# Attention logits on the two halves of TensorE's rows, with the decay added by VectorE

## The chip, the cores and the metric

The kernel runs on one core of one Trainium2 chip. A core has a matrix engine (TensorE, PE in the profile; PEld is its loading of weights), a vector engine (VectorE, DVE), a scalar engine (ScalarE, ACT), GpSimd (POOL) and SyncE (SP, which here issues most of the DMAs). TensorE reads SBUF and writes PSUM, a memory of banks of 512 f32 columns; VectorE and ScalarE read PSUM and clear it for the next use. Each engine works through its own queue in order and waits on semaphores.

The metric is device time in microseconds, the median over runs of the whole kernel.

## The reference

Two layers over 1024 positions of width 1024, each with a pre-norm and a residual, then a final norm. The first is an RG-LRU layer. The second, which the change concerns, is attention with a forget gate, 16 heads of 64:

```python
q, k, v = ...                      # (1024, 16, 64) each, from h @ w_in
f_logit = u[..., 4 * 1024:] + b_f  # one gate value per position and head
cum = jnp.cumsum(jax.nn.log_sigmoid(f_logit), axis=1)
logits = einsum("bqhd,bkhd->bhqk", q, k) / 8
logits = logits + (cum[query] - cum[key])
logits = where(key <= query, logits, -1e30)
p = softmax(logits)
y = einsum("bhqk,bkhd->bqhd", p, v) * silu(gate)
x = x + y @ w_out
```

The term `cum[query]` is the same for all keys of a query, so it drops out of a softmax that subtracts the row's maximum; only `-cum[key]` matters.

## The kernel before

Every f32 operand of a product is split in two: `hi`, the value rounded to the type that TensorE multiplies at full pace (f32r), and `lo`, the rest (`to_hi`, `to_lo`). A product of two split operands is the sum of three: hi by hi, hi by lo, lo by hi. The projections (`gemm_steps`) issue these three for each of 8 blocks of the contraction, 512 columns at a time, into one PSUM bank. All products go through the helper at L54, so in the profile they are told apart by tile names: `gps` (projections), `ups` and `ops`, `vps` (values), `S` (logits), `pt` (transposes of p), `O` (weighted sums), `turn` (the last stage).

Attention goes head by head. The queries and keys of a pair of heads come out of `kq_units` as `qkh` and `qkl`, [128 x 1024], two heads on 64 partitions each. `load` and `load_q` copy one head's part by DMA, from SBUF to SBUF, into two sets of operands that alternate by head:

- `T[s]`, the keys, [128, 2, 1024]. Slab 0 has hi on rows 0 to 63 and lo on rows 64 to 127. Slab 1 has hi again on rows 0 to 63, and on rows 64 to 67 two rows of ones and the two parts of `cum`.
- `U[s][c]`, the queries of half c of the sequence, [128, 2, 512]. Slab 0 has hi on both halves of the rows. Slab 1 has lo on rows 0 to 63, and on rows 64 to 67 the two parts of `cum` and two rows of minus one.

`cum` is computed in `forget`, half by half, split into hi and lo by VectorE, and kept in DRAM (`cumd`). `fixed_rows` sets the constant rows once.

`maxima(hd, c)` makes the logits of four blocks of 128 queries. Block i has n = 128(i+1) keys, and they go into a PSUM tile `S` of two banks (tag "S", two buffers, which the transposes `pt` use too) in one or two pieces of 256 columns or more, each the sum of two products: slab 0 with all 128 rows (hi by hi and hi by lo), slab 1 with 96 rows (lo by hi, and the decay). Then VectorE (L715) adds a bf16 mask of n columns, negates, and finds the row's minimum `m`, all in one instruction, and ScalarE (L720) writes p = exp(-S + m) to SBUF with its row sums. `weigh(hd, c)` later transposes p on TensorE (L58), splits it (`ph` by ScalarE, `pl` by VectorE) and multiplies it with the values.

The order of the work is written by hand. `run(order, ...)` reads a string: 0 is a step of `weigh`, 1 a block of `maxima`, and a dot is a step of `fill`, six 512-column products of the projections for the next pair (in the last heads, of the output projection), as in `ORDER = "1.0.1.1.1.0.0", "10.1.0.1.01.0.0"`. Each step is issued behind the last product of the step before. `load(hd + 2)` stands at the end of head hd's steps. The last stage, `turned`, takes the buffers of `T`, `U` and `U0`, `U1` for its results, and a buffer "xp" for squares.

Of the kernel before, what the change touches and what calls it, by code (L numbers as in the profile page):

```python
# [11 lines left out]
F32 = mybir.dt.float32  # L12
# [5 lines left out]
P = 128  # L18
# [20 lines left out]
def trunk(ctx: ExitStack, tc: tile.TileContext, xt, w0, wg, wo0, pc, gn, gf, w1, wv, wf, bf, wo1, out):  # L39
# [33 lines left out]
    for _ in range(10):  # L73
        matmul(warm[:, :P], onesf, onesf, start=True, stop=True)

    pct = const.tile([P, 8, NB], F32, name="pct")
    gnt = const.tile([P, 2, KT], F32, name="gnt")
    cw = [pct[:, j] for j in range(4)]
    cb, ba, bx, ap_ = (pct[:, j] for j in range(4, 8))


    def to_hi(hi, src, eng, scale=None):
# [99 lines left out]
    late = ctx.enter_context(ExitStack())  # L182
    with ExitStack() as l0:
        xpool = l0.enter_context(pool("x", 1))
        ypool = l0.enter_context(pool("y", 2 * GROUP))
        lru = l0.enter_context(ExitStack())
        tmp = lru.enter_context(pool("t0", 1, side="right"))
# [6 lines left out]
            return tmp.tile([P, SEQ], dtype, tag=tag, name=tag, bufs=bufs)  # L194


        sm = const
        c2 = sm.tile([P, NB], F32, name="c2")
        nc2 = sm.tile([P, NB], F32, name="nc2")
        e_ = sm.tile([P, NB], F32, name="sp_e")  # L200
# [285 lines left out]


    y1d = dram.tile([2, KT, P, HALF], F32, name="y1d")
    cumd = dram.tile([HEADS, 2, SEQ], F32, name="cumd")
    recd = dram.tile([HEADS, 8, P], F32, name="recd")  # L490

    with ExitStack() as l1:
# [2 lines left out]

        T = [tu.tile([P, 2, SEQ], F32R, tag=f"T{s}", name=f"T{s}") for s in range(2)]

        U0 = tu.tile([P, 2, HALF], F32R, tag="U", name="U")  # L500
        U = [(U0, tu.tile([P, 2, HALF], F32R, tag=f"U{s}", name=f"U{s}")) for s in range(2)]

        def fixed_rows():
            for s in range(2):
                nc.gpsimd.memset(f32(T[s][64:, 1]), 1.0)
                for u in U[s][s:]:
                    nc.vector.memset(f32(u[64:, 1]), 0.0)
                    nc.vector.memset(f32(u[64:68, 1]), -1.0)

        def project(w, use, hs=(0, 1)):  # L510

# [87 lines left out]
        def load(hd, cs=slice(0, SEQ), us=(0, 1)):  # L599

            pair, s = hd // 2, hd % 2
            rows = slice(s * HD, (s + 1) * HD)
            hi, lo = (f32(z[rows, cs]) for z in kq[pair, 1])
            nc.sync.dma_start(f32(T[s][:64, 0, cs]), hi)
            nc.sync.dma_start(f32(T[s][:64, 1, cs]), hi)
            nc.sync.dma_start(f32(T[s][64:, 0, cs]), lo)
            nc.sync.dma_start(f32(T[s][66:68, 1, cs]), cumd[hd, :, cs])
            for c in us:
                load_q(hd, c)

        def load_q(hd, c):
            s = hd % 2
            u = U[s][c]
            hi, lo = (f32(z[s * HD : (s + 1) * HD, halves[c]]) for z in kq[hd // 2, 0])
            nc.sync.dma_start(f32(u[:64, 0]), hi)
            nc.sync.dma_start(f32(u[64:, 0]), hi)
            nc.sync.dma_start(f32(u[:64, 1]), lo)
            nc.sync.dma_start(f32(u[64:66, 1]), cumd[hd, :, halves[c]])


        drain(kq_units(0, ((1, (0,)), (0, (0,)))))
# [3 lines left out]
        Vs = {}  # L625
        bft = const.tile([HEADS, 1], F32, name="bft")
        nc.sync.dma_start(bft, bf)
        unit = at.tile([HEADS, HALF], F32, tag="recb", name="unit", bufs=1)
        nc.gpsimd.memset(unit, 1.0)
        cum = at.tile([HEADS, SEQ], F32, tag="sg", name="cum")  # L630

        def forget(half):
            cs = slice(half * HALF, (half + 1) * HALF)
            pt = ps.tile([P, HALF], F32, tag="O", name="fps")
            for i in range(4):
                if half and i > 1:
                    yield
                with tc.issue_after(pe[0].ins):
                    transpose(pt[:HEADS, i * P : (i + 1) * P], fz[:, half * 4 + i], ident)
            z_, e_ = (at.tile([HEADS, HALF], F32, tag=t, name=n, bufs=3) for t, n in (("ph", "z"), ("pl", "e")))  # L640
            parts = [at.tile([HEADS, HALF], F32R, tag=f"p{i + 2 * half}", name="cp", bufs=1) for i in (3, 4)]
            hi, lo = parts
            nc.scalar.activation(z_, pt[:HEADS], AF.Identity, bias=bft)
            nc.vector.scalar_tensor_tensor(e_, z_, -1.0, z_, ALU.mult, ALU.min)
            nc.scalar.activation(e_, e_, AF.Exp)
            nc.scalar.activation(e_, e_, AF.Ln, bias=1.0)
            nc.vector.scalar_tensor_tensor(z_, z_, 0.0, e_, ALU.min, ALU.subtract)
            nc.vector.tensor_tensor_scan(
                cum[:, cs], unit, z_, cum[:, HALF - 1 : HALF] if half else 0.0, ALU.mult, ALU.add
            )  # L650
            to_hi(hi, cum[:, cs], nc.vector)
            to_lo(lo, cum[:, cs], hi, nc.vector)
            for i in range(2):
                nc.sync.dma_start(cumd[:, i, cs], f32(parts[i]))
            for hd in range(2):
                if half == 0:
                    load(hd, cs, (0,) if hd == 0 else ())
# [2 lines left out]
        next(first)  # L660
        next(first)

        fixed_rows()

        mask = tu.tile([P, SEQ], BF16, name="mask")
        nc.gpsimd.memset(mask, 0.0)
        nc.gpsimd.affine_select(
            out=mask, in_=mask, pattern=[[-1, SEQ]], compare_op=ALU.is_ge, fill=NEG, base=SEQ - P, channel_multiplier=1
        )

        take(first, 8)
# [20 lines left out]
        def maxima(hd, c):  # L692

            s = hd % 2
            pair = hd // 2
            if c == 0:
                stats[hd] = at.tile([P, 8], F32, tag="sums", name="sums")
            sums = stats[hd]
            for i in range(4 * c, 4 * c + 4):
                n = (i + 1) * P  # L700

                o_ = 192 if i == 4 else 0
                S = ps.tile([P, SEQ], F32, tag="S", name="S")[:, o_:]
                u = U[s][c]
                qs = slice(i % 4 * P, i % 4 * P + P)
                for lo_, hi_ in ((0, min(n, HALF - o_)), (HALF - o_, n)):
                    if hi_ <= lo_:
                        continue
                    hi_ = max(hi_, lo_ + 256)
                    matmul(S[:, lo_:hi_], u[:, 0, qs], T[s][:, 0, lo_:hi_], start=True, stop=False)  # L710
                    matmul(
                        S[:, lo_:hi_], u[:96, 1, qs], T[s][:96, 1, lo_:hi_], start=False, stop=True
                    )
                m = at.tile([P, 1], F32, tag="m", name="m", bufs=4)
                nc.vector.tensor_tensor_reduce(  # L715
                    S[:, :n], S[:, :n], mask[:, SEQ - n :], -1.0, -NEG, ALU.add, ALU.min, accum_out=m
                )

                p = ps_[i] = at.tile([P, n], F32, tag=f"p{i}", name="p", bufs=1)
                seen[0] = nc.scalar.activation(  # L720
                    p, S[:, :n], AF.Exp, bias=m, scale=-1.0, accum_out=sums[:, i : i + 1]
                )
                yield
            if hd == HEADS - 1 or c == 1:
                b0, b1 = (4 * c if hd == HEADS - 1 else 0), 4 * c + 4
                nb = b1 - b0
                sums = sums[:, b0:b1]
                nc.vector.tensor_scalar(sums, sums, 2.0, None, ALU.mult)
                nc.vector.reciprocal(sums, sums)
                tr = ps.tile([P, P], F32, tag="O", name="tr")  # L730
                nc.tensor.transpose(tr[:nb], sums, ident)
                rc = at.tile([8, P], F32, tag="rc", name="rc", bufs=1)
                nc.vector.tensor_copy(rc[:nb], tr[:nb])
                nc.gpsimd.dma_start(recd[hd, b0:b1], rc[:nb])
                if s == 0:
                    recs[pair] = at.tile([P, SEQ], F32, tag="recb", name="recb", bufs=1)
                rows = slice(s * HD, (s + 1) * HD)
                nc.gpsimd.dma_start(
                    recs[pair][rows, b0 * P : b1 * P],
                    recd[hd : hd + 1, b0:b1].rearrange("o b q -> o (b q)").to_broadcast([HD, nb * P]),  # L740
                )
                yield
# [155 lines left out]
        def turned(c, q):  # L898
# [2 lines left out]
            xs = left.pop((c, q), None) or residual(c, q)  # L901

            if c == 0:
                res = tu.tile([P, 2, SEQ], F32, tag=f"T{q}", name="res")
                res = [res[:, b] for b in range(2)]
            elif q == 0:
                res = [tu.tile([P, SEQ], F32, tag=t, name="res") for t in ("U", "U0")]
            else:
                res = [tu.tile([P, SEQ], F32, tag="U1", name="res"), at.tile([P, SEQ], F32, tag="p7", name="res", bufs=1)]
            for b in range(2):  # L910
# [4 lines left out]
                for h, (d0, nd) in enumerate(parts):  # L915
# [6 lines left out]
                    for k in range(2):  # L922
# [4 lines left out]
                        matmul(pt, yh, wl, start=False, stop=k == 1)  # L927
                        if k == 0:
                            yield
                    sq = at.tile([P, HALF], F32, tag="xp", name="sq1", bufs=2)[:, : nd * P]  # L930
                    nc.scalar.activation(sq, pt, AF.Square, accum_out=ss[:, min(h, ss.shape[1] - 1)].unsqueeze(1))
                    if c == 0 or h < len(parts) - 1:
                        nc.vector.tensor_tensor(res[b][:, hs], pt, grow[:, hs], ALU.mult)
# [189 lines left out]
```

## Time and profile before

| | |
|---|---|
| median of 3 runs | 1125.76 us (1124.42 to 1128.13) |
| the profiled execution, first to last instruction | 1127.7 us |
| TensorE busy | 1114.3 us, 99% |
| VectorE busy | 758.6 us, 67% |
| ScalarE busy | 589.3 us, 52% |
| GpSimd busy | 195.6 us, 17% |
| granted TensorE clock, mean | 0.998 |
| first and last product into S start at | 504.2 and 1072.7 us |

The profile is one execution, recorded by the hardware; its span lies inside the range of the runs, 1.9 us above their median. In a row of a group, the first number behind the bar is the time in which at least one of the group ran, then follows the mean length of one in ns, then the engine's idle time ahead of the group and what ended it. Products are pipelined and their ends are modelled, so two of them overlap in the record; their starts tell the pace.

### The profile page before, as it was taken

How to read it: one execution, taken by the hardware profiler on the slowest of the kernel's cores; microseconds unless marked ns; L12 is line 12 of the kernel's file. 1: busy time of each engine (PE TensorE's matmuls, PEld its weight loads, DVE VectorE, ACT ScalarE, POOL GpSimd, SP SyncE). 2: the span in 40 equal slices, each digit the busy share in tenths (PEclk: the TensorE clock that was granted, in tenths of full speed). 3: DMA queues.
4: the chain of work that ended last, by engine and by line, in shares of the span. 5: the costliest groups of instructions: out<-in, count | busy, mean ns of one | idle time of the engine just before them, and what ended most of it. 6: DMA issues, size and time to landing. Idle time of an engine off the chain costs nothing.

```text
span 1127.7 us, 15774 instructions
## 1 busy us (share of the span) xinstructions
PE 1114.3 (99%) x5691; PEld 936.8 (83%) x5691; DVE 758.6 (67%) x1268; ACT 589.3 (52%) x1081; POOL 195.6 (17%) x155
## 2 busy tenths in 40 slices
PE   9999999999999999999999999999999999999997
PEld 7788888888888887988888988889888898888786
DVE  7888755776568789656676466664667646676545
ACT  8488345355453656365555355553555535644335
POOL 1322112221121201431021110212102110021220
PEclk9999999999999999999999999999999999999999
DMA  6111111111111114433425224242252422564345
GB/s 235 57 47 42 51 52 52 38 58 45 52 38 52 47 44 145 129 112 102 112 71 123 66 77 117 72 118 71 74 119 73 118 71 77 176 189 158 117 154 187
DMA packets 62902, 105.43 MB, mean 93 GB/s; under 512 B 9796, under 2 KB 24772, under 8 KB 62824
## 3 DMA queue, kind: packets, MB, share of 16 engines
q1 hardware_dynamic: 59704, 95.97, 28.9%
q0 software_dynamic: 3120, 8.46, 2.3%
q8 instruction: 45, 0.74, 0.3%
q14 instruction: 33, 0.27, 0.1%
HBM read 63.30 MB, written 15.93 MB: 70 GB/s over the span
## 4 chain that ended last, share of the span: by engine, by line
PE 92%; DMA 2%; DVE 2%; issue 1%; ACT 1%; SPq 1%; POOL 0%; DVEq 0%; POOLq 0%; ACTq 0%
PE gps L54 33%; PE ops L54 16%; PE ups L54 12%; PE vps L54 8%; PE S L54 6%; PE O L54 6%; PE pt L58 5%; PE gate L54 3%; PE turn L54 3%; DMA wf<-in_wo 1%; DMA x<-in_xt 1%; POOL wl L96 0%; PE rsrow L54 0%; DMA wf<-in_w 0%; DMA yhl<-y1d 0%
## 5 line engine op out<-in xcount | busy, mean ns | idle before, releaser
L54 PE MATMUL gps<-hh,wh 128*128 128x512 f32 x576 | 229.1, 398 | 0.6 <-DVE qkl L595 0.6
L54 PE MATMUL gps<-hh,wl 128*128 128x512 f32 x576 | 226.8, 394 | 0.0
L54 PE MATMUL gps<-hl,wh 128*128 128x512 f32 x576 | 226.7, 394 | 0.0
L85 ACT CAST wh<-wf 128x512 fp32r<-128x512 f32 (+2 forms) x156 | 94.2, 607 | 147.8 <-PE ops L54 55.3
L96 POOL TENSOR_TENSOR wl<-wf,wh 128x512 fp32r<-128x512 f32 (+1 forms) x60 | 101.0, 1689 | 389.8 <-ACT wh L85 362.5
L720 ACT ACTIVATE p<-S,m 128x128 f32<-128x128 f32 (+7 forms) x128 | 94.8, 741 | 137.9 <-DVE m L715 136.8
L96 DVE TENSOR_TENSOR pl<-pt,ph 128x512 fp32r<-128x512 f32 (+1 forms) x198 | 98.7, 540 | 88.1 <-ACT ph L85 87.6
L54 PEld LDWEIGHTS gps<-hl,wh 128*128 128x128 f32 x576 | 108.3, 188 | 24.7 <-issue 0.5
L54 PEld LDWEIGHTS gps<-hh,wh 128*128 128x128 f32 x576 | 108.6, 189 | 20.5 <-DVE qkl L595 0.8
L54 PEld LDWEIGHTS gps<-hh,wl 128*128 128x128 f32 x576 | 108.7, 189 | 20.1 <-POOL wl L96 0.6
L715 DVE CUSTOM_DVE_ANT_0 S<-S,mask 128x128 f32<-128x128 f32 (+7 forms) x128 | 97.3, 761 | 28.8 <-PE S L54 28.8
L85 ACT CAST ph<-pt 128x512 fp32r<-128x512 f32 (+1 forms) x198 | 83.6, 473 | 36.2 <-PE pt L58 28.9
L54 PE MATMUL S<-T,U 96*128 96x512 f32 (+7 forms) x384 | 91.9, 348 | 2.7 <-ACT p L720 2.7
L96 DVE TENSOR_TENSOR wl<-wf,wh 128x512 fp32r<-128x512 f32 x96 | 70.7, 741 | 28.3 <-ACT wh L85 27.4
L381 DVE TENSOR_TENSOR x<-x,ops 128x512 f32<-128x512 f32 x80 | 54.1, 683 | 48.0 <-PE ops L54 48.0
L54 PEld LDWEIGHTS S<-T,U 128*128 128x128 f32 (+1 forms) x384 | 68.6, 190 | 16.1 <-ACT p L720 3.5
L58 PE MATMUL pt<-ident,p 128*128 128x128 f32 x576 | 79.4, 273 | 0.8 <-DVE pl L96 0.5
L58 PEld LDWEIGHTS pt<-ident,p 128*128 128x128 f32 x576 | 67.2, 140 | 13.9 <-issue 2.9
L54 PE MATMUL ups<-hh,wh 128*128 128x512 f32 x192 | 76.1, 397 | 1.1 <-ACT hh L87 1.1
L54 PE MATMUL ups<-hl,wh 128*128 128x512 f32 x192 | 76.7, 399 | 0.2
L54 PE MATMUL ops<-yh,wh 128*128 128x512 f32 x192 | 76.0, 396 | 0.5 <-DVE x L474 0.5
L54 PE MATMUL ups<-hh,wl 128*128 128x512 f32 x192 | 76.2, 397 | 0.0
(183 smaller groups left out, 2247.8 us busy)
## 6 DMA issues: line engine op xcount, KB each, us to landing
wf<-in_w SPq DMA_DIRECT2D x100, 256.0 KB
wf<-in_wo SPq DMA_DIRECT2D x64, 128.0 KB
U<-qkh SPq DMA_DIRECT2D x64, 128.0 KB
T<-qkh SPq DMA_DIRECT2D x28, 256.0 KB
x<-in_xt SPq DMA_DIRECT2D x16, 256.0 KB
x1d<-x SPq DMA_DIRECT2D x16, 256.0 KB
wf<-in_wv SPq DMA_DIRECT2D x16, 256.0 KB
U<-qkl SPq DMA_DIRECT2D x32, 128.0 KB
```

What stands on the lines that cost most here:

```text
L54: pe[0] = nc.tensor.matmul(*args, **kw)
L58: pe[0] = nc.tensor.transpose(*args)
L85: nc.scalar.copy(hi, src)
L96: return eng.tensor_tensor(lo, src, f32(hi), ALU.subtract)
L381: nc.vector.tensor_tensor(x, x, pt, ALU.add)
L715: nc.vector.tensor_tensor_reduce(S[:, :n], S[:, :n], mask[:, SEQ - n :], -1.0, -NEG, ALU.add, ALU.min, accum_out=m)
L720: seen[0] = nc.scalar.activation(p, S[:, :n], AF.Exp, bias=m, scale=-1.0, accum_out=sums[:, i : i + 1])
```

## The change

The contraction of a logit is only 64 long, so 64 of TensorE's 128 rows hold it. Before, the other 64 rows held the second term and the decay. After the change they hold the same term for other keys. The n keys of a block are cut in two halves of n/2 = 64(i+1). Rows 0 to 63 of `T` have the left keys (0 to 511), rows 64 to 127 the right keys (64 to 1023, stored 64 to the left); slab 0 is hi, slab 1 is lo. `U` has each query part on both halves of the rows. A block is then six products of 64 rows and n/2 columns, in this order: lo by hi, left and right; hi by lo, left and right; hi by hi, left and right. The view of `S` starts at column 512 - n/2, so that the left keys end where the first bank ends and the right keys begin where the second begins.

The decay is no longer part of the products. `forget` computes the negated sum, writes it unsplit to `cumd` [16, 1024], and `load` spreads one head's row to all 128 partitions of `decay[s]`. VectorE adds a mask to the last 128 columns, in an instruction of its own, and the reduction reads `decay` in place of the bf16 mask. `fixed_rows` is gone. The constants of the first layer (`pct` and the tiles of its softplus) move to the pool of that layer; in `turned`, results take the buffers of `T` and `decay`, and the squares those of `pl`.

```diff
--- before.py
+++ after.py
...
@@ -486,7 +486,7 @@
 
 
     y1d = dram.tile([2, KT, P, HALF], F32, name="y1d")
-    cumd = dram.tile([HEADS, 2, SEQ], F32, name="cumd")
+    cumd = dram.tile([HEADS, SEQ], F32, name="cumd")
     recd = dram.tile([HEADS, 8, P], F32, name="recd")
 
     with ExitStack() as l1:
@@ -495,17 +495,11 @@
 
 
 
-        T = [tu.tile([P, 2, SEQ], F32R, tag=f"T{s}", name=f"T{s}") for s in range(2)]
+        T = [tu.tile([P, 2, SEQ - 64], F32R, tag=f"T{s}", name=f"T{s}") for s in range(2)]
 
         U0 = tu.tile([P, 2, HALF], F32R, tag="U", name="U")
+        decay = [tu.tile([P, SEQ], F32, tag=f"d{s}", name=f"d{s}") for s in range(2)]
         U = [(U0, tu.tile([P, 2, HALF], F32R, tag=f"U{s}", name=f"U{s}")) for s in range(2)]
-
-        def fixed_rows():
-            for s in range(2):
-                nc.gpsimd.memset(f32(T[s][64:, 1]), 1.0)
-                for u in U[s][s:]:
-                    nc.vector.memset(f32(u[64:, 1]), 0.0)
-                    nc.vector.memset(f32(u[64:68, 1]), -1.0)
 
         def project(w, use, hs=(0, 1)):
 
@@ -600,22 +594,22 @@
 
             pair, s = hd // 2, hd % 2
             rows = slice(s * HD, (s + 1) * HD)
-            hi, lo = (f32(z[rows, cs]) for z in kq[pair, 1])
-            nc.sync.dma_start(f32(T[s][:64, 0, cs]), hi)
-            nc.sync.dma_start(f32(T[s][:64, 1, cs]), hi)
-            nc.sync.dma_start(f32(T[s][64:, 0, cs]), lo)
-            nc.sync.dma_start(f32(T[s][66:68, 1, cs]), cumd[hd, :, cs])
+            for j, z in enumerate(kq[pair, 1]):
+                if cs.start == 0:
+                    nc.sync.dma_start(f32(T[s][:64, j, :HALF]), f32(z[rows, :HALF]))
+                right = slice(max(cs.start, 64), cs.stop)
+                nc.sync.dma_start(f32(T[s][64:, j, right.start - 64 : right.stop - 64]), f32(z[rows, right]))
+            nc.sync.dma_start(decay[s][:, cs], cumd[hd : hd + 1, cs].to_broadcast([P, cs.stop - cs.start]))
             for c in us:
                 load_q(hd, c)
 
         def load_q(hd, c):
             s = hd % 2
             u = U[s][c]
-            hi, lo = (f32(z[s * HD : (s + 1) * HD, halves[c]]) for z in kq[hd // 2, 0])
-            nc.sync.dma_start(f32(u[:64, 0]), hi)
-            nc.sync.dma_start(f32(u[64:, 0]), hi)
-            nc.sync.dma_start(f32(u[:64, 1]), lo)
-            nc.sync.dma_start(f32(u[64:66, 1]), cumd[hd, :, halves[c]])
+            for j, z in enumerate(kq[hd // 2, 0]):
+                z = f32(z[s * HD : (s + 1) * HD, halves[c]])
+                for rows in (slice(0, 64), slice(64, P)):
+                    nc.sync.dma_start(f32(u[rows, j]), z)
 
 
         drain(kq_units(0, ((1, (0,)), (0, (0,)))))
@@ -625,6 +619,7 @@
         Vs = {}
         bft = const.tile([HEADS, 1], F32, name="bft")
         nc.sync.dma_start(bft, bf)
+        nc.vector.tensor_scalar(bft, bft, -1.0, None, ALU.mult)
         unit = at.tile([HEADS, HALF], F32, tag="recb", name="unit", bufs=1)
         nc.gpsimd.memset(unit, 1.0)
         cum = at.tile([HEADS, SEQ], F32, tag="sg", name="cum")
@@ -638,20 +633,15 @@
                 with tc.issue_after(pe[0].ins):
                     transpose(pt[:HEADS, i * P : (i + 1) * P], fz[:, half * 4 + i], ident)
             z_, e_ = (at.tile([HEADS, HALF], F32, tag=t, name=n, bufs=3) for t, n in (("ph", "z"), ("pl", "e")))
-            parts = [at.tile([HEADS, HALF], F32R, tag=f"p{i + 2 * half}", name="cp", bufs=1) for i in (3, 4)]
-            hi, lo = parts
-            nc.scalar.activation(z_, pt[:HEADS], AF.Identity, bias=bft)
+            nc.scalar.activation(z_, pt[:HEADS], AF.Identity, bias=bft, scale=-1.0)
             nc.vector.scalar_tensor_tensor(e_, z_, -1.0, z_, ALU.mult, ALU.min)
             nc.scalar.activation(e_, e_, AF.Exp)
             nc.scalar.activation(e_, e_, AF.Ln, bias=1.0)
-            nc.vector.scalar_tensor_tensor(z_, z_, 0.0, e_, ALU.min, ALU.subtract)
+            nc.vector.scalar_tensor_tensor(z_, z_, 0.0, e_, ALU.max, ALU.add)
             nc.vector.tensor_tensor_scan(
                 cum[:, cs], unit, z_, cum[:, HALF - 1 : HALF] if half else 0.0, ALU.mult, ALU.add
             )
-            to_hi(hi, cum[:, cs], nc.vector)
-            to_lo(lo, cum[:, cs], hi, nc.vector)
-            for i in range(2):
-                nc.sync.dma_start(cumd[:, i, cs], f32(parts[i]))
+            nc.sync.dma_start(cumd[:, cs], cum[:, cs])
             for hd in range(2):
                 if half == 0:
                     load(hd, cs, (0,) if hd == 0 else ())
@@ -660,12 +650,10 @@
         next(first)
         next(first)
 
-        fixed_rows()
-
-        mask = tu.tile([P, SEQ], BF16, name="mask")
+        mask = tu.tile([P, P], F32, name="mask")
         nc.gpsimd.memset(mask, 0.0)
         nc.gpsimd.affine_select(
-            out=mask, in_=mask, pattern=[[-1, SEQ]], compare_op=ALU.is_ge, fill=NEG, base=SEQ - P, channel_multiplier=1
+            out=mask, in_=mask, pattern=[[-1, P]], compare_op=ALU.is_ge, fill=NEG, base=0, channel_multiplier=1
         )
 
         take(first, 8)
@@ -699,21 +687,18 @@
             for i in range(4 * c, 4 * c + 4):
                 n = (i + 1) * P
 
-                o_ = 192 if i == 4 else 0
-                S = ps.tile([P, SEQ], F32, tag="S", name="S")[:, o_:]
+                half = n // 2
+                S = ps.tile([P, SEQ], F32, tag="S", name="S")[:, HALF - half :]
                 u = U[s][c]
                 qs = slice(i % 4 * P, i % 4 * P + P)
-                for lo_, hi_ in ((0, min(n, HALF - o_)), (HALF - o_, n)):
-                    if hi_ <= lo_:
-                        continue
-                    hi_ = max(hi_, lo_ + 256)
-                    matmul(S[:, lo_:hi_], u[:, 0, qs], T[s][:, 0, lo_:hi_], start=True, stop=False)
-                    matmul(
-                        S[:, lo_:hi_], u[:96, 1, qs], T[s][:96, 1, lo_:hi_], start=False, stop=True
-                    )
+                for t, (j, l) in enumerate(((1, 0), (0, 1), (0, 0))):
+                    for r, (rows, ks) in enumerate(((slice(0, 64), slice(0, half)), (slice(64, P), slice(half, n)))):
+                        ts = T[s][rows, l, ks.start - 64 * r : ks.stop - 64 * r]
+                        matmul(S[:, ks], u[rows, j, qs], ts, start=t == 0, stop=t == 2)
                 m = at.tile([P, 1], F32, tag="m", name="m", bufs=4)
+                nc.vector.tensor_tensor(S[:, n - P : n], S[:, n - P : n], mask, ALU.add)
                 nc.vector.tensor_tensor_reduce(
-                    S[:, :n], S[:, :n], mask[:, SEQ - n :], -1.0, -NEG, ALU.add, ALU.min, accum_out=m
+                    S[:, :n], S[:, :n], decay[s][:, :n], -1.0, -NEG, ALU.add, ALU.min, accum_out=m
                 )
 
                 p = ps_[i] = at.tile([P, n], F32, tag=f"p{i}", name="p", bufs=1)
@@ -901,8 +886,7 @@
             xs = left.pop((c, q), None) or residual(c, q)
 
             if c == 0:
-                res = tu.tile([P, 2, SEQ], F32, tag=f"T{q}", name="res")
-                res = [res[:, b] for b in range(2)]
+                res = [tu.tile([P, SEQ], F32, tag=f"{t}{q}", name="res") for t in "Td"]
             elif q == 0:
                 res = [tu.tile([P, SEQ], F32, tag=t, name="res") for t in ("U", "U0")]
             else:
@@ -927,7 +911,7 @@
                         matmul(pt, yh, wl, start=False, stop=k == 1)
                         if k == 0:
                             yield
-                    sq = at.tile([P, HALF], F32, tag="xp", name="sq1", bufs=2)[:, : nd * P]
+                    sq = at.tile([P, HALF], F32, tag="pl", name="sq1", bufs=3)[:, : nd * P]
                     nc.scalar.activation(sq, pt, AF.Square, accum_out=ss[:, min(h, ss.shape[1] - 1)].unsqueeze(1))
                     if c == 0 or h < len(parts) - 1:
                         nc.vector.tensor_tensor(res[b][:, hs], pt, grow[:, hs], ALU.mult)
```

More of the change, by code (lines that the diff above doesn't have):

```diff
@@ L74, in trunk @@
         matmul(warm[:, :P], onesf, onesf, start=True, stop=True)
-    pct = const.tile([P, 8, NB], F32, name="pct")
     gnt = const.tile([P, 2, KT], F32, name="gnt")
-    cw = [pct[:, j] for j in range(4)]
-    cb, ba, bx, ap_ = (pct[:, j] for j in range(4, 8))
     def to_hi(hi, src, eng, scale=None):
@@ L184, in trunk @@
         xpool = l0.enter_context(pool("x", 1))
+        pct = xpool.tile([P, 8, NB], F32, name="pct")
+        cw = [pct[:, j] for j in range(4)]
+        cb, ba, bx, ap_ = (pct[:, j] for j in range(4, 8))
         ypool = l0.enter_context(pool("y", 2 * GROUP))
@@ L194, in long @@
             return tmp.tile([P, SEQ], dtype, tag=tag, name=tag, bufs=bufs)
-        sm = const
+        sm = xpool
         c2 = sm.tile([P, NB], F32, name="c2")
```

## The prediction

> **What bounds the kernel now.** I began with the page: busy shares, the chain, then the logits' groups and their pace in the timeline.
>
> ```profile
> PE 1114.3 (99%) x5691; PEld 936.8 (83%) x5691; DVE 758.6 (67%) x1268; ACT 589.3 (52%) x1081; POOL 195.6 (17%) x155
> PE 92%; DMA 2%; DVE 2%; issue 1%; ACT 1%; SPq 1%; POOL 0%; DVEq 0%; POOLq 0%; ACTq 0%
> PE gps L54 33%; PE ops L54 16%; PE ups L54 12%; PE vps L54 8%; PE S L54 6%; PE O L54 6%; PE pt L58 5%; PE gate L54 3%; PE turn L54 3%; DMA wf<-in_wo 1%; DMA x<-in_xt 1%; POOL wl L96 0%; PE rsrow L54 0%; DMA wf<-in_w 0%; DMA yhl<-y1d 0%
> ```
>
> TensorE is busy 99% of the span and is 92% of the chain; the products into S, which the change rewrites, are 6% of it. Whatever TensorE gains or loses there reaches the end almost whole. The windows answer, split at the end of attention (start and end, length, then busy us of each engine, clock, DMA share), says the same, and shows VectorE at 369 of 580 us:
>
> ```profile
> 500.00:1080.00 580.00, 575.91 (x3212) 495.79 (x3211) 368.69 (x767) 289.86 (x655) 84.70 (x78) 1.00 0.38 106
> 1080.00:1128.00 48.00, 41.36 (x244) 34.97 (x242) 24.09 (x55) 21.69 (x61) 4.93 (x7) 0.98 0.51 176
> ```
>
> Now what the pieces cost. A "mean ns of one" includes latency that the next product overlaps, so I use the distance between starts. First the groups kept apart by shape, then the TensorE timeline (start, length, product, count) at five places.
>
> ```profile
> L54 PE MATMUL S<-T,U 128*128 128x512 f32 x80 | 31.7, 397 | 2.7 <-ACT p L720 2.7
> L54 PEld LDWEIGHTS S<-T,U 96*128 96x128 f32 x192 | 36.5, 190 | 6.0
> L54 PEld LDWEIGHTS S<-T,U 128*128 128x128 f32 x192 | 36.3, 189 | 10.1 <-ACT p L720 3.5
> ```
>
> ```profile
> 439.70 1.84 PE L54 MATMUL sscol<-onesf,sq 128*128 128x1 f32 x16
> 441.40 0.48 PE L54 MATMUL gps<-hh,wh 128*128 128x512 f32 x1
> ...
> 516.21 0.86 PE L54 MATMUL S<-T,U 128*128 128x512 f32 x4
> 516.91 0.40 PE L54 MATMUL gps<-hh,wh 128*128 128x512 f32 x1
> 517.14 0.40 PE L54 MATMUL gps<-hh,wl 128*128 128x512 f32 x1
> ...
> 541.24 0.28 PE L54 MATMUL O<-ph,v 128*128 128x256 f32 x1
> 541.36 0.28 PE L54 MATMUL O<-pl,v 128*128 128x256 f32 x1
> 541.47 0.22 PE L54 MATMUL O<-ph,v 128*128 128x128 f32 x1
> 541.53 0.28 PE L54 MATMUL O<-pl,v 128*128 128x128 f32 x1
> 541.64 0.81 PE L54 MATMUL S<-T,U 128*128 128x320 f32 x4
> ...
> 905.15 0.51 PE L54 MATMUL S<-T,U 128*128 128x384 f32 x2
> 905.50 0.40 PE L54 MATMUL gps<-hh,wh 128*128 128x512 f32 x1
> ```
>
> A 512-column product takes 0.23 (516.91 to 517.14); one of 384 takes 0.175 (two in 905.15 to 905.50); by the line through these, 256 takes 0.12 (0.12 from 541.24), 320 takes 0.148, 448 takes 0.203. The check: two of 512 and two of 256 take 0.70 (516.21 to 516.91). Sixteen one-column products take 1.70 (439.70 to 441.40), so a product with its own weight load costs at least 0.106 to 0.11 however few its columns; I use 0.11. Two 128-column products take 0.17 (541.47 to 541.64): nothing is charged for being narrow. A load of 96 rows takes the 190 ns of one of 128 rows.
>
> **The logits, term by term.** Before, per head, blocks i = 0 to 7 cost 0.24, 0.24, 0.35, 0.46, 0.59, 0.70, 0.81, 0.92 (two products per piece; pieces of 256, 256, 384, 512, 2x320, 512+256, 512+384, 2x512), 4.31 together, 69.0 us for 16 heads. After, block i has six products of s = 64(i+1) columns: three terms, each on rows 0 to 63 for the left keys and rows 64 to 127 for the right keys. That is 768 products and 768 loads in place of 384. No row of this trace has a product on half the rows, so I bound it from both sides:
>
> - Lower end: the two products of a term, loads included, run side by side. A term takes max(0.11, s's pace): 0.11 three times, then 0.12, 0.148, 0.175, 0.203, 0.23, sum 1.206; three terms and 16 heads make 57.9, a change of -11.1.
> - Upper end: nothing overlaps. A term takes twice that, 115.8 in all, +46.8.
> - Between: the halves stream side by side (other rows, and other banks: the left keys end where the second bank begins), but the loads still pass one after the other at 0.11. A term then takes max(0.22, s's pace). The first two loads fit under the 0.23 of the product ahead, and after the last term only the next product's load remains, so a block is 2 x max(0.22, s) + max(0.11, s): 0.55 three times, 0.56, 0.588, 0.615, 0.643, 0.69, sum 4.75, 75.9 in all, +6.9.
>
> I take the middle. The only measured fact about partial rows is that a 96-row load costs what a 128-row one does, and the nearest pace of loads is the 0.11 of the one-column run; streams of disjoint rows share nothing that a row shows.
>
> **VectorE.** Added: 128 adds of the 128x128 mask, one per block, between the products and the reduction. Reading S with the f32 decay instead of the bf16 mask is free: the 1024-wide reduction is as long as an add of two f32 operands.
>
> ```profile
> L96 DVE TENSOR_TENSOR pl<-pt,ph 128x128 fp32r<-128x128 f32 x33 | 9.3, 281 | 0.0
> L715 DVE CUSTOM_DVE_ANT_0 S<-S,mask 128x1024 f32<-128x1024 f32 x16 | 19.7, 1232 | 6.1 <-PE S L54 6.1
> L289 DVE TENSOR_TENSOR us<-ups,rs 128x1024 f32<-128x1024 f32 x11 | 13.4, 1221 | 4.4 <-PE ups L54 4.4
> ```
>
> 128 x 0.281 = 36.0, VectorE in attention from 369 to 405 of 580 us (70%). It is off the path; the cover is the fill product work between S blocks. Behind each add wait the reduction, the exponential on ScalarE, and the S buffer that both a later S block and the transposes (pt) need. How near that is to biting, in the waits view (total, times, longest):
>
> ```profile
> ACT p L720 <- DVE m L715: 136.8, 94, 2.9
> PE S L54 <- ACT p L720: 2.7, 1, 2.7
> PEld S L54 <- ACT p L720: 3.5, 2, 3.1
> PE pt L58 <- ACT p L720: 0.3, 1, 0.3
> ```
>
> ScalarE waits for VectorE 94 times, but TensorE waited for the exponential hardly at all. Ends: 0, and 36.0 if every add is exposed. I take 2, near the waits.
>
> **The front and the queues.** Gone: the split of the cumulative sum (two casts, two subtractions), six memsets on VectorE, two on POOL; the mask shrinks.
>
> ```profile
> 503.15 0.40 DVE L91 CAST cp<-cum 16x512 fp32r<-16x512 f32 x1
> 504.08 0.67 DVE L96 TENSOR_TENSOR cp<-cum,cp 16x512 fp32r<-16x512 f32 x1
> 505.41 0.50 PE L54 MATMUL gps<-hh,wh 128*128 128x512 f32 x1 [0.59 <-DVE qkl L595]
> ```
>
> These stand ahead of a qkl for which TensorE was idle 0.59: gain between 0 and 0.59, I take 0.5. With them gone, the next thing late there is the weight split in VectorE's queue. On SP a full load was 4+8 transfers and becomes 5+8; at half 1 of the first two heads it falls from 8 to 7, at half 0 it gains one. Per head T goes from 776 to 736 KB, the queries from 776 to 1024 KB, and the decay, spread to 128 partitions, adds 512 KB: +720 KB, 11.5 MB in all over
>
> ```profile
> q1 hardware_dynamic: 59704, 95.97, 28.9%
> T<-qkh SPq DMA_DIRECT2D x28, 256.0 KB
> U<-qkh SPq DMA_DIRECT2D x64, 128.0 KB
> ```
>
> that is 12% more on a queue at 29% of the engines, issued a head ahead of use. Cover: the previous head's whole work; nil cost (without the cover, one landing per head). The decay of a slot is freed by a reduction rather than by a product, still half a head before its reload. In the last layer the squares move to the buffers of pl, which the last weighted sums use: hidden while fill remains, 0 here. The constants that move pools, and the negated bias, cost nothing.
>
> **The sum.** 1127.7 + 6.9 + 2 - 0.5 = 1136.1 of span. That execution's span lies 1.9 above the median 1125.76 of the runs, and I take the same off: 1134.
>
> **The rivals.** First, on the other side: loads of the two halves also go side by side. For it: nothing in the half products shares rows, and the loads of S are 190 ns long yet 0.11 apart, so the load path already overlaps in itself. Against: no load starts closer than 0.106 to another here. The time is 1127.7 - 11.1 + 1.5 - 1.9 = 1116. What decides is the pace of a pair of half products: setting the per-head sum of the middle formula to 4.31 less 0.09 for the other terms gives about 0.18; a pair below that is a gain, above it a loss.
>
> The Trainium skill, "TensorE: Matmul & The Clock Gate", Part 3 (packing small matmuls), says that products on different row groups run concurrently, starting about 4 ns apart, and that a load overlaps products in flight only where row groups differ. By that rule the sum would be the first rival's. The second half of the rule does not agree with this trace, where every 128-row load already runs under the product before it (83% PEld beside 99% PE).
>
> Second: each entry to and exit from half-row work empties the array. There are 128 blocks, thus 256 switches. Price from rows: a 512-column product is 0.397 long but the next starts 0.23 later, so 0.167 of it is hidden; if a switch exposes that, 256 x 0.167 = 42.8. On top of the first rival this gives 1159, on top of my middle 1177. For it: nothing before ever leaves full height except the 96-row products, and these (0.175 beside their 128-row partners) show no such cost, which speaks mildly against.
>
> The Trainium skill, "TensorEngine Tiling (Array Packing)", Key Properties, says that changing the tiling mode drains TensorE; that is this second rival, and no run so far shows it.
>
> Third: nothing overlaps, 1127.7 + 46.8 + 1.5 - 1.9 = 1174. For it: no two products overlap in their streams anywhere in this trace. Against: they all use the same rows.
>
> Fourth: the adds are exposed in full, 34 more than my 2: 1168. Against: the few waits above.
>
> **How the numbers follow.** Chances: middle 0.32, first rival 0.27, drain 0.24, no overlap 0.11, exposed adds 0.06. The predicted time is the middle's 1134; its own range is 1127 to 1143. The 8-in-10 range goes from 1114 (the first rival with no stall) to 1176 (no overlap, and most of the drain cases); I leave out some 6 in 100 below and 12 above. About 0.3% is what a measurement of this kernel can tell from no change, so faster means below 1122.4. Faster 0.25 (the first rival less its stalled cases), same 0.06 (the edges of it and of the middle), slower 0.69.
>
> **What would show it.** In the timeline, a 256-column block (i = 3) as six products in about 0.56 says middle; 0.36 the first rival; 0.72 no overlap. A product after S starting over 0.1 later than its own pace says drain. The S loads 0.11 apart say the loads bind; starts of pairs within some ns say that streams overlap. The adds should be 0.28 each, the reductions as long as before, and TensorE's waits for p a few us. I am wrong if pairs pace below 0.18, if the gap at each block's edge is large, or if TensorE's idle before S or pt grows past 5 us.

## The result and the profile after

The changed kernel takes 1173.93 us (1173.41 to 1176.80), the kernel before 1126.16 us beside it; the ratio is 1.0429, with a 95% interval of 1.0406 to 1.0452. It is slower, some 48 us of it. The time is inside the range of the prediction, but the forecast was 8 us.

The spans of executions lie 1.7 to 1.8 us under their times. The first profile of the kernel before has a span of 1127.7, more than those of all but one of its timed runs; a second profile, further down, has 1122.2 and is the fair one to compare with 1171.8.

First the page after: busy shares and the chain.

```profile
span 1171.8 us, 16725 instructions
PE 1151.9 (98%) x6075; PEld 923.2 (79%) x6075; DVE 799.1 (68%) x1387; ACT 587.2 (50%) x1081; POOL 192.5 (16%) x153
PE 87%; ACT 4%; DVE 4%; DMA 2%; issue 2%; SPq 1%; ACTq 0%; DVEq 0%
```

TensorE is still the bound and some 40 us busier than in the second profile of the kernel before (1112.1). ScalarE and VectorE have come into the chain with 4% each; before, they had 1% and 2%. So two things are new: more TensorE time, and waits for the way from S to p.

Now one block of seven eighths of the keys (i = 6, six products of 448 columns), as the timeline of TensorE shows it (start, length, product, count, and the idle time ahead of it in brackets).

```profile
518.62 0.39 PE L54 MATMUL gps<-hh,wl 128*128 128x512 f32 x1
518.84 0.40 PE L54 MATMUL gps<-hl,wh 128*128 128x512 f32 x1
519.17 0.87 PE L54 MATMUL S<-T,U 64*128 64x448 f32 x6
519.98 0.50 PE L54 MATMUL gps<-hh,wh 128*128 128x512 f32 x1
520.31 0.39 PE L54 MATMUL gps<-hh,wl 128*128 128x512 f32 x1
```

The six products take 0.81 from their first start to the next product's. Six products one after the other would take 6 x 0.203 = 1.22; three pairs side by side 0.61. So the halves do run together, and 0.20 is lost inside the block. There is more around it: the projection product ahead takes 0.33 (518.84 to 519.17) where its like takes 0.23, and the one behind takes 0.33 too (519.98 to 520.31). In all the block costs 0.81 + 0.10 + 0.10 = 1.01, 0.40 above its three pairs. Below, an unbroken run of half-row products among full-height ones is called a visit, and this loss at its two ends the cost of its edges.

The same place cut off at 519.30, with the weight loads:

```profile
518.62 0.19 PEld L54 LDWEIGHTS gps<-hl,wh 128*128 128x128 f32 x1
519.17 0.30 PEld L54 LDWEIGHTS S<-T,U 64*128 64x128 f32 x4 [0.36 <-issue]
519.17 0.47 PE L54 MATMUL S<-T,U 64*128 64x448 f32 x2
```

Two products and four loads have started within 0.13. One load is 0.186 long in the groups below; four, each 0.11 behind the one before, would be busy for 0.52, and these are for 0.30. So the loads of the two halves run side by side too, in two pairs 0.11 apart; the products of a pair start 3 to 5 ns apart in this block. And no load of a half-row product starts before 519.17, although the load path had been idle for 0.36: the load that otherwise runs under the product ahead is not issued. The groups of the loads say it for all blocks; the last columns are the idle time of the load path and what ended it. After:

```profile
L54 PEld LDWEIGHTS gps<-hh,wh 128*128 128x128 f32 x576 | 108.0, 188 | 37.8 <-issue 14.3 <-ACT v L84 0.6 <-ACT wh L82 0.4
L54 PEld LDWEIGHTS S<-T,U 64*128 64x128 f32 x768 | 56.7, 186 | 45.5 <-ACT p L705 20.3 <-issue 15.4 <-ACT ph L82 5.8
```

Before (the second profile):

```profile
L54 PEld LDWEIGHTS gps<-hh,wh 128*128 128x128 f32 x576 | 108.4, 188 | 21.0 <-DVE qkl L595 1.2
L54 PEld LDWEIGHTS S<-T,U 128*128 128x128 f32 x192 | 36.3, 189 | 7.0 <-ACT p L720 0.4
```

768 loads are busy for 56.7 us in all, less than 384 were (36.3 and, for the 96-row ones, 36.5). The new idle time is "issue", 15 us ahead of the loads for S and 14 ahead of the first projection load behind a block, where nothing that the profile shows is waited for; and 20.3 us ahead of S for the exponential of an earlier block, where 0.4 stood. That second part belongs to VectorE, whose rows after are:

```profile
L699 DVE TENSOR_TENSOR S<-S,mask 128x128 f32<-128x128 f32 x128 | 37.9, 296 | 25.7 <-PE S L54 24.7
L700 DVE CUSTOM_DVE_ANT_0 S<-S,d 128x1024 f32<-128x1024 f32 x16 | 19.7, 1233 | 0.6
```

The added mask is 0.296 a piece, and the reduction with the f32 decay is as long as with the bf16 mask (1233 against 1232 ns).

### The profile page after: what moved, and what is told of

Its sections match the earlier page's. It is cut to its first block, busy times and chain, and to the rows that moved or that the text cites. A ratio compares the mean times of both kernels' runs of the same rounds, so it can differ in the third digit from the quotient of the medians.

```text
span 1171.8 us, 16725 instructions
## 1 busy us (share of the span) xinstructions
PE 1151.9 (98%) x6075; PEld 923.2 (79%) x6075; DVE 799.1 (68%) x1387; ACT 587.2 (50%) x1081; POOL 192.5 (16%) x153
## 4 chain that ended last, share of the span: by engine, by line
PE 87%; ACT 4%; DVE 4%; DMA 2%; issue 2%; SPq 1%; ACTq 0%; DVEq 0%
PE gps L54 28%; PE ops L54 16%; PE ups L54 11%; PE vps L54 8%; PE S L54 6%; PE O L54 6%; PE pt L58 5%; PE gate L54 3%; PE turn L54 3%; ACT ph L82 2%; ACT p L705 1%; DVE wl L93 1%; DMA wf<-in_w 1%; DVE pl L93 1%; DMA U<-qkh 1%
## 5 line engine op out<-in xcount | busy, mean ns | idle before, releaser
L54 PE MATMUL gps<-hh,wh 128*128 128x512 f32 x576 | 238.9, 415 | 0.1
L82 ACT CAST ph<-pt 128x512 fp32r<-128x512 f32 (+1 forms) x198 | 86.3, 473 | 89.7 <-PE pt L58 84.4
L700 DVE CUSTOM_DVE_ANT_0 S<-S,d 128x128 f32<-128x128 f32 (+7 forms) x128 | 97.8, 764 | 3.6
L93 DVE TENSOR_TENSOR wl<-wf,wh 128x512 fp32r<-128x512 f32 x96 | 80.2, 839 | 22.2 <-ACT wh L82 21.2
L54 PE MATMUL S<-T,U 64*128 64x64 f32 (+7 forms) x768 | 89.7, 339 | 5.6 <-ACT p L705 4.7
L54 PEld LDWEIGHTS S<-T,U 64*128 64x128 f32 x768 | 56.7, 186 | 45.5 <-ACT p L705 20.3
L381 DVE TENSOR_TENSOR x<-x,ops 128x512 f32<-128x512 f32 x80 | 54.1, 683 | 48.7 <-PE ops L54 48.6
L54 PE MATMUL ops<-yh,wl 128*128 128x512 f32 x192 | 75.6, 394 | 0.1
```

The lines of the kernel that those rows point to most:

```text
L54: pe[0] = nc.tensor.matmul(*args, **kw)
L82: nc.scalar.copy(hi, src)
L93: return eng.tensor_tensor(lo, src, f32(hi), ALU.subtract)
L381: nc.vector.tensor_tensor(x, x, pt, ALU.add)
L700: nc.vector.tensor_tensor_reduce(S[:, :n], S[:, :n], decay[s][:, :n], -1.0, -NEG, ALU.add, ALU.min, accum_out=m)
```

## The experiments

The theory with which I went on: the halves overlap completely (-11.1 us); every visit to half-row work costs about 0.39 us at its edges, 50 us for 128 blocks (126 visits in this trace, where two blocks twice stand side by side); the longer way from S to p costs some us of waits. The rivals: the added VectorE instruction holds TensorE up, and the products cost nothing; or the products do not overlap and the edges cost nothing, which would come to +47 and so fit the time as well.

**The products alone.** The kernel before, with the six half-row products, their operands and loads (`T` keeps its size), and no decay; the reduction adds the bf16 mask as before.

```diff
-                    matmul(S[:, lo_:hi_], u[:, 0, qs], T[s][:, 0, lo_:hi_], start=True, stop=False)
-                    matmul(S[:, lo_:hi_], u[:96, 1, qs], T[s][:96, 1, lo_:hi_], start=False, stop=True)
+                for t, (j, l) in enumerate(((1, 0), (0, 1), (0, 0))):
+                    for r, (rows, ks) in enumerate(((slice(0, 64), slice(0, half)), (slice(64, P), slice(half, n)))):
+                        ts = T[s][rows, l, ks.start - 64 * r : ks.stop - 64 * r]
+                        matmul(S[:, ks], u[rows, j, qs], ts, start=t == 0, stop=t == 2)
```

> The kernel before with the products alone changed: six products of 64 rows per block, keys on the two halves of the rows; the decay is left out of the logits, and the reduction adds the bf16 mask as before, so VectorE has no added instruction. My theory now (the halves run side by side, and every entry to and exit from half-row products costs 0.39 us per block, as the trace of the changed kernel reads): 1126 - 11 + 50 = 1165, between 1158 and 1170. Rival 1, the added mask instruction on VectorE holds TensorE up: near 1115, since it isn't there. Rival 2, the halves don't overlap but nothing is lost at the edges: 1126 + 47 = 1173.

Measured: 1158.94 us against 1123.90, ratio 1.0313 (1.0298 to 1.0327), 35.0 us more. With -11.1 for the columns, which this run does not show by itself, that leaves 46.1, which is 0.36 per visit. The rival without these products' cost (1115) is out. The rival without overlap (1173) is 14 too high, and the rows above show the overlap itself.

**The decay alone.** The changed kernel with products of full height: slab 1 has zeros on rows 64 to 95 in place of the decay. (For space the mask is bf16, and a small tile of the gate uses another buffer.)

```diff
-                        matmul(S[:, ks], u[rows, j, qs], ts, start=t == 0, stop=t == 2)
+                    matmul(S[:, lo_:hi_], u[:, 0, qs], T[s][:, 0, lo_:hi_], start=True, stop=False)
+                    matmul(S[:, lo_:hi_], u[:96, 1, qs], T[s][:96, 1, lo_:hi_], start=False, stop=True)
```

> The changed kernel with the products of before: 128 and 96 rows, with zeros where the decay was; the decay and the mask are added by VectorE as in the changed kernel. My theory: TensorE's work is as before and the longer way from S to p costs some waits for the S buffer, 3 to 8 us: 1129 to 1134. Rival 1, each added instruction is exposed: 1126 + 36 = 1162. Rival 2 (only the products matter): 1126.

Measured: 1141.41 us, ratio 1.0156 (1.0142 to 1.0170), 17.5 us more. That is neither the few us of my theory nor the 36 of full exposure: about half of the added VectorE time shows.

**One more visit per block.** Two kernels add the same product to the changed one, 128 rows by 64 columns of zeros into S. In the control it stands behind the six, next to a full-height product; in the other it stands after the fourth of the six.

```diff
                         matmul(S[:, ks], u[rows, j, qs], ts, start=t == 0, stop=t == 2)
+                    if t == 1:
+                        matmul(S[:, half - 64 : half], u[:, 0, qs], zero, start=False, stop=False)
```

> The changed kernel with one more product per block behind its six: 128 rows, 64 columns of zeros, added into S. It stands beside the full-height product that follows anyhow, so it adds no entry or exit. All theories: 128 x 0.11 = 14 more than the changed kernel, 1188; it is the control of the next.

> The same added product, but after the fourth of the six, so that each block leaves half-row work and enters it again once more. My theory: 128 x 0.39 = 50 above the control, 1238. Rival 2 (no cost of the switch): as the control, 1188. Rival 1 (VectorE): as the control.

Measured: 1184.66 us behind the six, 1223.88 in their middle. The same work in another place costs 39.2 us more, 0.31 per added visit, a fifth less than the 0.39 that I had expected. This is the clearest of the runs: neither the columns, nor the loads, nor VectorE differ.

**Before once more, the mask left out, and fewer or other visits.** First the kernel before, for the second profile.

> The kernel before once more, for a second profile of it: the first one's span of 1127.7 us lies above the spans of its timed runs (1121.7 and 1122.1 us for times of 1123.4 and 1123.8), and holds one wait of TensorE for an exponential of near 3 us. Expected: a span near 1122 without that wait, and otherwise the same pace of every product.

Measured: 1123.95 us, span 1122.2. Its waits of the load path (total, times, longest) have nothing longer than 1.4 us, and the wait of 3 us is gone:

```profile
PEld pt L58 <- issue: 3.0, 8, 0.4
PEld ups L54 <- ACT hh L87: 2.2, 3, 1.4
```

In the next run the add of the mask is taken out of the changed kernel (later keys then stay in the softmax).

```diff
-                nc.vector.tensor_tensor(S[:, n - P : n], S[:, n - P : n], mask, ALU.add)
```

> The changed kernel with the separate add of the mask left out (so later keys are not masked); the decay is still added in the reduction. The decay alone cost 17.5 us on the full-height kernel. If that is the added 0.28 us on VectorE ahead of each reduction, this run comes out 10 to 17 us below the changed kernel's 1174, near 1160. If it is the added transfers (decay rows spread to 128 partitions, 720 KB per head), it stays at 1174.

Measured: 1159.74 us, ratio 1.0308 (1.0277 to 1.0339), so some 14 us (give or take 4, by the two intervals) below the changed kernel and level with the products alone (1.0313), although all its added transfers are still there. The transfers cost nothing that can be seen; the one instruction does. The longest waits of its load path:

```profile
PEld S L54 <- issue: 17.3, 48, 0.4
PEld S L54 <- ACT ph L82: 14.9, 41, 0.4
PEld gps L54 <- issue: 14.7, 53, 0.4
PEld S L54 <- ACT p L704: 1.9, 3, 1.2
```

The last line, from further down the list, is the wait of S for an exponential: 20.3 us in the changed kernel, 1.9 here. The idle time at the edges has stayed. (The 14.9 at "ACT ph" are 41 pieces of at most 0.4 us. I read them as edges too, put down to the semaphore that came last; the trace does not prove it.)

In the third, the blocks 0, 1 and 2, 3 of a head go as pairs into one S tile, twelve half-row products in a row.

```diff
+                if c == 1 or i % 2 == 0:
+                    S2 = ps.tile([P, 2, HALF], F32, tag="S", name="S")
...
+                    for b in (i, i + 1)[: 2 - c]:
...
+                                matmul(V[:, r], u[rows, j, qs], ts, start=t == 0, stop=t == 2)
```

> The changed kernel with the blocks i = 0, 1 and i = 2, 3 of a head issued as pairs, their twelve half-row products in a row into one S tile; the second block's VectorE and ScalarE work stays at its own step. That is 96 visits to half-row work in place of 128. My theory: 32 visits saved at 0.31 (the added visit of the middle product) to 0.39 us (the edges of a block in the trace), 10 to 12.5 us below 1174, near 1162, unless waits for S change. Without a cost of visits: 1174.

Measured: 1162.42 us, ratio 1.0334 (1.0299 to 1.0369). 32 visits fewer have given back about 0.0095 of 1124, 10.7 us, 0.33 each; by the two intervals this is good to some 5 us, or 0.15 each.

In the fourth no two half-row products stand side by side. It is the kernel with the decay alone, its second product cut from 96 rows (32 of them zeros) to 64.

```diff
-                    matmul(S[:, lo_:hi_], u[:96, 1, qs], T[s][:96, 1, lo_:hi_], start=False, stop=True)
+                    matmul(S[:, lo_:hi_], u[:64, 1, qs], T[s][:64, 1, lo_:hi_], start=False, stop=True)
```

> The kernel with the decay alone, whose second product of each piece (96 rows, of which 32 are zeros) has 64 rows, so no two half-row products stand side by side. 192 pieces, each now entering and leaving half-row work. My theory, the visit itself costs: 192 x 0.31 to 0.39 = 59 to 75 above 1141, 1200 to 1216. If a visit costs only where two halves run together, or the edge cost was the start of the pair: 1141.

Measured: 1207.76 us, 66.4 above the decay alone. That is 0.35 for each of 192 visits, for products that do less than before. The loads by form:

```profile
L54 PEld LDWEIGHTS S<-T,U 128*128 128x128 f32 x192 | 36.1, 188 | 23.7 <-issue 14.3 <-ACT p L708 4.2 <-DMA U<-qkl 0.2
L54 PEld LDWEIGHTS S<-T,U 64*128 64x128 f32 x192 | 35.2, 183 | 46.1 <-issue 40.4
```

The 64-row loads now come after 46.1 us of idle time, 40.4 of it "issue"; 96-row loads came after 6.0. A lone product on 64 rows pays; one on 96 does not.

**The VectorE instruction by itself.** Two more runs put an instruction of 128 columns into the kernel before. In the first it adds zeros to S ahead of the reduction; in the second it works on a tile that no later instruction of attention reads, and is written behind the reduction.

```diff
+                nc.vector.tensor_tensor(S[:, n - P : n], S[:, n - P : n], mask[:, :P], ALU.add)
                 nc.vector.tensor_tensor_reduce(
                     S[:, :n], S[:, :n], mask[:, SEQ - n :], -1.0, -NEG, ALU.add, ALU.min, accum_out=m
                 )
```

```diff
                 nc.vector.tensor_tensor_reduce(
                     S[:, :n], S[:, :n], mask[:, SEQ - n :], -1.0, -NEG, ALU.add, ALU.min, accum_out=m
                 )
+                nc.vector.tensor_tensor(onesf, onesf, mask[:, :P], ALU.add)
```

> The kernel before with one VectorE instruction more per block: zeros (128 columns of the mask that are zero) are added to the last 128 columns of S between the products and the reduction. Products, transfers and decay are those of before. If the 17.5 us of the decay part come from that one instruction, this costs 13 to 18 us: 1137 to 1142. If they come from the transfers or the f32 operand of the reduction, it costs under 4.

> The same instruction on an SBUF tile that nothing waits for, issued behind the reduction, so that VectorE is as busy but S to p is no longer on its own account. If the cost is the longer way from S to p (the S buffer comes free 0.28 us later), this costs 0 to 5 us: 1124 to 1129. If it is VectorE's load in general, it costs as much as the one ahead of the reduction.

Measured: ahead of the reduction 1143.37 us, ratio 1.0148 (1.0113 to 1.0183), some 17 us more; on the other tile 1132.25 us, ratio 1.0064 (1.0042 to 1.0085), some 7 us more. So the whole cost of the decay part can come from that one instruction ahead of the reduction.

The second run does not answer its question, for its trace shows that the instruction did not run behind the reductions. The first line has its 128 pieces with their first and last start, the second a wait of TensorE:

```profile
L718 DVE TENSOR_TENSOR onesf<-onesf,mask x128: 254/291/2493, 469.5 to 566.0; 128x128 f32<-128x128 f32 x128
502.00 0.50 PE L54 MATMUL gps<-hh,wh 128*128 128x512 f32 x1 [3.07 <-DVE qkl L96]
```

Nothing ties these adds to a block. They ran between 469.5 and 566.0, each ahead of the reduction behind which it is written, and 62 of them before the first reduction at all. The loss lies there too: against the second profile of the kernel before, the first reduction starts 6.3 us later, the 33rd 8.4, and the last 8.5. So the 7 us are the price of a crowd of adds at the front, and how the 17 us of the first run divide between VectorE's load and the instruction's place between S and p stays open.

In the first run the loss grows through all of attention: the 17th reduction starts 1.5 us later than in the second profile, the 105th 11.6, and the last 20.8, so nearly half falls into the last three heads. The waits of the load path there:

```profile
PEld S L54 <- ACT p L721: 7.5, 17, 1.0
PEld pt L58 <- DVE pl L96: 5.8, 4, 1.8
PEld pt L58 <- ACT p L721: 3.9, 2, 2.8
```

In the kernel before (the second profile) the first of them was:

```profile
PEld S L54 <- ACT p L720: 0.4, 1, 0.4
```

S waits for the exponential that frees its buffer 17 times in place of once, and the transposes, which share the buffers, wait as well, for the exponential and for VectorE's split of p.

## Why the prediction was right or wrong

The sign and the bound held: TensorE stayed at 98%, and what happened in its products reached the end. The size did not: 8 us forecast, 48 measured. That the range held was luck. Its upper end came from the rival without overlap. That rival's 1174 equals the measured time by chance, for the halves do overlap.

**The step that failed is "I take the middle".** It was meant as the value between two ends, with loads in line at 0.11, and the trace of the changed kernel shows loads of the two halves side by side. It priced the products at +6.9 and their edges at nothing; measured, the products alone cost +35.0. The lower end, -11.1, was right for the columns, as far as the larger blocks show: from 256 to 448 columns (0.56 below and 0.81 above) a block grows by 0.25, three times the 0.083 by which one product's pace grows, where six in line would have grown by 0.50. The 0.20 that is left inside is the same for both. The reason I gave against it, that no load starts closer than 0.106 to another, was drawn from products that all use the same rows. The measured fact that I leaned on, the 96-row load, does not bear on half-height work at all.

**A cost at each switch, the drain, was a rival at 0.24, and such a cost is what the runs show.** Its price was 0.167 per switch, 42.8 us in all; measured are 0.31 to 0.36 us per visit, that is 0.16 to 0.18 per switch, and 46 in all in the kernel with the products alone. So the price came out near, and the chance was wrong. Whether the price came out for the reason that I gave, the part of a product that the next one hides, no run shows. What I held mildly against it, that the 96-row products show no such cost, was true and beside the point: cutting those 96 rows to 64 brought the cost at once (66.4 us). The Trainium skill, "TensorEngine Tiling (Array Packing)", Key Properties, says that changing the tiling mode drains TensorE. The 0.31 us of the added visit and the 0.35 of the lone 64-row products agree with a loss at each change; that it is the array emptying they do not show. The Trainium skill, "TensorE: Matmul & The Clock Gate", Part 3, says that products on different row groups run concurrently; the three pairs in 0.81 us, edges included, agree.

**The second term that failed is the 2 us for VectorE's adds.** They cost 17.5 alone and 14 in the changed kernel. I took the cover from the waits of TensorE for the exponential, a few us in the trace before. Those told that nothing was late then, not how little it took to be late: a fill step between two blocks is 1.4 us, and 0.29 more in front of an exponential that frees one of two buffers made 17 waits of S where there had been one. The other end, 36, was further off still.

Put together, -11.1 + 46.1 + 13.6 = 48.6, for a measured 48 (1.0429 x 1126 less 1126); 13.6 is the difference of the ratios with and without the mask add, times 1124. The first two terms add up to the 35.0 of the products alone by construction, so what this sum tests is that the kernel without the mask add (1.0308) and the products alone (1.0313) agree.

**Right in the parts:** the reduction with an f32 operand costs nothing; the added transfers cost nothing, though they are 11.5 MB; the add is 0.296 for the 0.281 assumed; narrow products are not charged. The front's term, -0.5, held in the trace: TensorE's wait for that qkl, 0.59 in the first profile of the kernel before and 0.96 in the second, is gone in the changed kernel. It is too small to be seen in the time.

**The signs I had named** were half good. A block of 256 columns was to take 0.56 in the middle case, 0.36 in the first rival. In the changed kernel:

```profile
571.31 0.40 PE L54 MATMUL O<-pl,v 128*128 128x512 f32 x1
571.63 0.62 PE L54 MATMUL S<-T,U 64*128 64x256 f32 x6
572.19 0.50 PE L54 MATMUL gps<-hh,wh 128*128 128x512 f32 x1
572.52 0.40 PE L54 MATMUL gps<-hh,wl 128*128 128x512 f32 x1
```

It takes 0.56, and for the wrong reason: 0.36 of pairs and 0.20 of edges. The sign for the drain, a product after S that starts over 0.1 later than its own pace, decided it: the product behind this block starts 0.20 later than three pairs would let it, and the one behind that 0.10 late (0.33 for 0.23). The sign of overlap held: the two products of a pair start 3 ns apart in the median. So did a sign of being wrong, TensorE's idle time before S or pt past 5 us: in the changed kernel its products wait 4.7 and 2.7 us for the exponential there, and its loads for S 20.3.

What stays open: what the engine does in the 0.31 to 0.36 us. The trace shows that loads for the other height are not issued under the product ahead, and that each edge is 0.16 to 0.20 long; it does not show whether products in flight must leave the array first, or only the weights must wait.

## What to carry to other kernels

Packing two half-height products side by side worked here as hoped, loads included, but each visit to half-height work among full-height products cost about 0.35 us, so the packed stretch has to save more than that at a time. Here the largest block saved 0.23 (0.92 to 0.69, by the pace of the columns), so none could pay for its own visit. The two largest of a head together would have saved 0.43 (1.73 to 1.30), hardly more than one visit costs, and one S tile doesn't hold both. And an instruction put between a PSUM tile's products and the instruction that frees the tile does not become free because the engine is busy for only 64% of the stretch: count how long the buffers may be late. The kernel before had its mask inside the reduction, which is as long with it as with the decay (1232 and 1233 ns).

## What the runs showed of the hardware that I had not expected

- Weight loads of 64-row products on rows 0 to 63 and on rows 64 to 127 run at the same time: four loads in 0.30 us, where full-height loads follow one another at 0.106 to 0.11 us.
- A visit to 64-row work among 128-row products cost 0.31 us (added in the middle of a block), 0.33 (blocks paired), 0.35 (lone 64-row products) and 0.36 (six per visit). A 96-row product among 128-row ones cost nothing that shows (two of 512 and two of 256 columns, half of them on 96 rows, in 0.70 us, which is the pace of 0.23 and 0.12 of such products on 128 rows).
- A VectorE instruction of 0.29 us between a block's products and its reduction, 128 times, cost some 17 us of a kernel in which VectorE is busy 67% of the time. The same number of adds that no block waits for ran in a crowd at the front, between 469.5 and 566.0 us, and cost 7.
